# A hybrid decoder layer on one core: the modulation's sums over partitions moved behind the next projection, their stream given its own slots, and one half projection moved forward

## The chip, the core and the metric

One core of a Trainium2 chip runs the whole layer as one program. The metric is the device time of one execution in microseconds (us); below it is better. PE is TensorE, DVE VectorE, ACT ScalarE, POOL GpSimd, and SP the engine that issues the DMAs.

## What is computed

The layer takes a sequence `x` of 1024 tokens by 1024 features and a conditioning vector `c`. The reference, cut to what matters here:

```python
mod = (c @ w_c + b_c).reshape(B, 6, D)
shift_m, scale_m, gate_m, shift_f, scale_f, gate_f = mod      # rows m = 0 to 5
u = x * (1.0 + scale_m) + shift_m
fq, fk, fv, ff, gq, gk, gv, ga, gr = split(u @ w_in)
fox_out = fox_attention(fq, fk, fv, ff, b_f)
gla_out = gla_attention(gq, gk, gv, ga, w_a2, b_a, gr, g_gla)
y = concatenate([fox_out, gla_out]) @ w_o
x = layer_norm(ALPHA * x + (1.0 + gate_m) * y, ln1_g, ln1_b)
u2 = x * (1.0 + scale_f) + shift_f
x = layer_norm(ALPHA * x + (1.0 + gate_f) * (silu(u2 @ w_gate) * (u2 @ w_up)) @ w_down, ln2_g, ln2_b)
```

All of it is float32. The kernel keeps that precision by splitting each operand into a high and a low part and multiplying three times (high by high, high by low, low by high).

## The kernel before

The work is unrolled in Python: a first stage computes the rows m = 0 and 1 of the modulation, the scaled input `u` (split into `uh` and `ul`) and part of the projections; then come the other projections, the linear heads (GLA), the softmax heads (FoX), the mixer and the feed-forward part.

**The projections in question.** `proj_tok` (L316) loads the weights of some columns in two halves with `load_split` (L90): a DMA on SP into a tile of kind `raw` (L92), a cast to the high part on ACT (L87), a subtraction for the low part on DVE (L88). `raw`, `hi` and `lo` are kinds of tiles with three buffers each. Then it runs over the eight token tiles in two groups of four banks, three matmuls for each of the eight blocks of features (L330 to L332), and evacuates. It is called four times in a row: gv0 and gv1 (264 columns each), gr0 and gr1 (256 each; their evacuation is the `gr` activation of L410).

**The rest of the modulation.** Between these calls stands `mod_rest(m)` for m = 2 to 5 (L339). It streams eight tiles of `w_c` (L343) through slots 35 to 37 and accumulates them on DVE, weighted by `c` (L345, L347), into slot 28 or 29. The accumulated tile is split into slots 37 and 35. Four matmuls with a column of ones (L359, L360, tile `mps`, banks b6 and b7) then sum over the partitions; the result is copied by ACT (L366; for m = 2 and 5 added to `b_c` on DVE, L362) to the tile `grow` in slot 32 and stored to the HBM tensor `grow_d` (L367). After `mod_rest(5)`, `mod_cols` (L369) loads the rows of m = 3 and 4 back into a `raw` tile (L371) and transposes them into columns (L373, tile `mcs`, bank b7).

**After the projections.** The low-rank gate input is transposed (L460, `gaps`, banks b6 and b7); `gla_prep` for two pairs of heads makes the decayed operands on DVE, ACT and POOL; then eight steps of `gla_pair` run, each for both pairs (among others the transposition `kt`, L534). The fq and fk projections of the softmax heads come in half projections, `units`, of 24 matmuls: two are called before the steps, and one behind each step while there are any (eight in all).

**What sets the order.** The framework takes the order of the program as priority. It simulates the program, and each engine gets its instructions in the order in which they are ready there, earlier ones in the program first. So a matmul may stand in PE's queue in front of others that precede it in the program. On the chip every queue is worked in order. A tile of a kind waits for a free buffer of that kind. `tc.issue_after(ins)` puts an instruction behind `ins` in the queue of its engine, without a wait for its end. The helper `after(key)` (L175) does that for the instruction remembered in `last[key]`.

Of the kernel before, what the change touches and what calls it, by code (L numbers as in the profile page):

```python
# [9 lines left out]
F32R = mybir.dt.float32r  # L10
# [8 lines left out]
NK = D // P  # L19
# [14 lines left out]
def hymba_layer_kernel(  # L34
# [21 lines left out]
    nc = tc.nc  # L56
# [13 lines left out]
    def nm(s):  # L70
        uid[0] += 1
        return f"{s}_{uid[0]}"

    def slot(i, shape=(1024,), dt=F32, name="t"):
        return sp.tile([P, *shape], dt, tag=f"s{i}", name=nm(name))

    def bank(tag, name="ps"):
        return pp.tile([P, 512], F32, tag=tag, name=nm(name))
# [7 lines left out]
    def split(dst_hi, dst_lo, src):  # L86
        nc.scalar.copy(dst_hi, src)  # L87
        return nc.vector.tensor_tensor(dst_lo, src, dst_hi.bitcast(F32), op=ALU.subtract).ins  # L88

    def load_split(shape, src):  # L90
        raw = wtile("raw", shape, F32)
        nc.sync.dma_start(raw, src)  # L92
        hi = wtile("hi", shape, F32R)
        lo = wtile("lo", shape, F32R)
        split(hi, lo, raw)
        return hi, lo
# [11 lines left out]
    ones_r = cp.tile([P, 1], F32R, name="ones_r")  # L108
# [28 lines left out]
    uh, ul = [], []  # L137
# [35 lines left out]
    last = {}  # L173

    def after(key):  # L175
        return tc.issue_after(last[key]) if key in last else nullcontext()
# [104 lines left out]
    for m in range(3):  # L281
        dst = [gq[0], gq[1], gk[0]][m]
        for h in range(2):
            hs = slice(h * 512, (h + 1) * 512)
# [9 lines left out]
    def pbank(n=4):  # L294
        pb[0] += 1
        return bank(f"b{pfirst[0] + pb[0] % n}", "acc")
# [19 lines left out]
    def proj_tok(col, n, nb, evac):  # L316
        ws = []
        for g in range(2):
            wv = w_in[g * 512 : (g + 1) * 512, col : col + n].rearrange("(k p) n -> p k n", p=P)
            ws.append(load_split((4, n), wv))  # L320
        per = 4 if nb >= 4 else 1
        for t0 in range(0, NT, per):
            pss = [pbank(nb) for _ in range(per)]
            for g in range(2):
                wh, wl = ws[g]
                for i in range(per):
                    ts = slice((t0 + i) * P, (t0 + i + 1) * P)
                    ps = pss[i][:, 0:n]
                    for k in range(4 * g, 4 * g + 4):
                        nc.tensor.matmul(ps, uh[k][:, ts], wh[:, k % 4, :], start=k == 0, stop=False)  # L330
                        nc.tensor.matmul(ps, uh[k][:, ts], wl[:, k % 4, :], start=False, stop=False)  # L331
                        nc.tensor.matmul(ps, ul[k][:, ts], wh[:, k % 4, :], start=False, stop=k == NK - 1)  # L332
            for i in range(per):
                evac(t0 + i, pss[i])

# [3 lines left out]
    def mod_rest(m):  # L339
        acc = slot(28 + m % 2, name="wacc")  # L340
        for k in range(NK):
            raw = slot(35 + k % 3, name="wc")
            nc.sync.dma_start(raw, w_c[k * P : (k + 1) * P, m * D : (m + 1) * D])  # L343
            if k == 0:
                nc.vector.tensor_scalar(acc, raw, ccol[:, 0:1], None, op0=ALU.mult)  # L345
            else:
                nc.vector.scalar_tensor_tensor(  # L347
                    acc, raw, ccol[:, k : k + 1], acc, op0=ALU.mult, op1=ALU.add
                )
        row = slot(32, name="grow")  # L350
        if m in (2, 5):
            nc.sync.dma_start(row[0:1, :], b_c[m * D : (m + 1) * D].rearrange("(o n) -> o n", o=1))
        hi = slot(37, dt=F32R, name="ah")
        lo = slot(35, dt=F32R, name="al")
        split(hi, lo, acc)
        for h in range(2):
            hs = slice(h * 512, (h + 1) * 512)
            ps = bank(f"b{6 + h}", "mps")
            nc.tensor.matmul(ps[0:1, :], ones_r, hi[:, hs], start=True, stop=False)  # L359
            nc.tensor.matmul(ps[0:1, :], ones_r, lo[:, hs], start=False, stop=True)  # L360
            if m in (2, 5):
                nc.vector.scalar_tensor_tensor(  # L362
                    row[0:1, hs], ps[0:1, :], 1.0, row[0:1, hs], op0=ALU.add, op1=ALU.add
                )
            else:
                nc.scalar.copy(row[0:1, hs], ps[0:1, :])  # L366
        nc.sync.dma_start(grow_d[m - 2 : m - 1, :], row[0:1, :])  # L367

    def mod_cols():  # L369
        rows = wtile("raw", (P,), F32)[0:16]  # L370
        nc.sync.dma_start(rows, grow_d[1:3, :].rearrange("m (k p) -> (m k) p", p=P))  # L371
        ps = bank("b7", "mcs")
        nc.tensor.transpose(ps[:, 0:16], rows, ident[0:16, 0:16])  # L373
        nc.vector.tensor_tensor(mcol[:, 2, :], ps[:, 0:8], cols[:, 24:32], op=ALU.add)
        nc.vector.scalar_tensor_tensor(mcol[:, 3, :], ps[:, 8:16], 1.0, cols[:, 32:40], op0=ALU.add, op1=ALU.add)

        nc.vector.tensor_tensor(mcol[:, 4, :], vcol[:, 16:24], mcol[:, 3, :], op=ALU.mult)
        nc.vector.tensor_tensor(mcol[:, 4, :], mcol[:, 2, :], mcol[:, 4, :], op=ALU.add)
        nc.vector.tensor_tensor(mcol[:, 5, :], mcol[:, 3, :], vcol[:, 8:16], op=ALU.mult)
# [12 lines left out]
    def evac_gv1(t, ps):  # L392
        nc.scalar.copy(gv_t(t)[:, 264:512], ps[:, 0:248])
        nc.scalar.copy(ga_tok[:, t, :], ps[:, 248:264])

    proj_tok(C_GV, 264, 4, evac_gv0)
    mod_rest(3)
    proj_tok(C_GV + 264, 264, 4, evac_gv1)
    mod_rest(4)

    gr = [slot(24 + i, (2, 512), name="gr") for i in range(4)]
# [3 lines left out]
    def gr_t(t):  # L405
        return gr[t // 2][:, t % 2, :]

    def evac_gr(h):
        def f(t, ps):
            nc.scalar.activation(gr_t(t)[:, h * 256 : (h + 1) * 256], ps[:, 0:256], AF.Silu)  # L410
            if h == 1:
                nc.gpsimd.tensor_tensor(gr_t(t), gr_t(t), ggb, op=ALU.mult)
        return f

    proj_tok(C_GR, 256, 4, evac_gr(0))
    mod_rest(5)
    mod_cols()
    proj_tok(C_GR + 256, 256, 4, evac_gr(1))


    def log_sigmoid(pss, bias, t0, t1, t2, n=P):
# [35 lines left out]
    for h in range(2):  # L457
# [3 lines left out]
        hs = slice(h * 512, (h + 1) * 512)  # L461
# [4 lines left out]
    def ch(t, i):  # L466
        return t.rearrange("p (n c t) -> p n c t", c=2, t=64)[:, :, i, :]
# [5 lines left out]
    def gla_prep(p):  # L473
        aps = []
        for h in range(2):
            hs = slice(h * 512, (h + 1) * 512)
            ps = bank(f"b{4 + h}", "aps")
            nc.tensor.matmul(ps, wa2[:, p * P : (p + 1) * P], gaT[0:80, hs], start=True, stop=True)
            aps.append(ps)
        t0, t1, t2 = gtmp[p]  # L480
        log_sigmoid(aps, vcol[:, p : 1 + p], t0, t1, t2)
        nc.vector.tensor_tensor_scan(t1, rmask, t0, 0.0, op0=ALU.mult, op1=ALU.add)
        bl = t1.rearrange("p (n t) -> p n t", t=64)[:, :, 63:64]
        nc.scalar.activation(t0, t1, AF.Exp, scale=1.0 / GATE_TEMP)
        nc.vector.tensor_tensor(gq[p], gq[p], t0, op=ALU.mult)
        nc.scalar.activation(t2, t1, AF.Exp, scale=-1.0 / GATE_TEMP)
        nc.vector.tensor_tensor(t2, gk[p], t2, op=ALU.mult)
        nc.scalar.activation(dec[:, p, :], bl.rearrange("p n t -> p (n t)"), AF.Exp, scale=1.0 / GATE_TEMP)
        nc.vector.tensor_tensor(
            t0.rearrange("p (n t) -> p n t", t=64),  # L490
            bl.broadcast_to([P, 16, 64]),
            t1.rearrange("p (n t) -> p n t", t=64),
            op=ALU.subtract,
        )
        nc.scalar.activation(t0, t0, AF.Exp, scale=1.0 / GATE_TEMP)
        nc.vector.tensor_tensor(gk[p], gk[p], t0, op=ALU.mult)
        d2 = dec[:, p, :].rearrange("p (n c) -> p n c", c=2)
        nc.vector.tensor_tensor(dec12[:, p, :], d2[:, :, 0], d2[:, :, 1], op=ALU.mult)
        nc.gpsimd.tensor_scalar(ch(t1, 0), ch(gk[p], 0), 1.0, 1.0, op0=ALU.mult, op1=ALU.mult)
        nc.gpsimd.tensor_scalar(ch(t1, 1), ch(t2, 1), 1.0, 1.0, op0=ALU.mult, op1=ALU.mult)  # L500
        nc.gpsimd.tensor_tensor(
            ch(gk[p], 0), ch(gk[p], 0), d2[:, :, 1:2].broadcast_to([P, 8, 64]), op=ALU.mult
        )
        nc.gpsimd.tensor_scalar(ch(t0, 0), ch(gq[p], 0), 1.0, 1.0, op0=ALU.mult, op1=ALU.mult)
        nc.gpsimd.tensor_tensor(
            ch(t0, 1), ch(gq[p], 1), d2[:, :, 0:1].broadcast_to([P, 8, 64]), op=ALU.mult
        )
# [68 lines left out]
    units = qk_units(0) + qk_units(1)  # L576
    gla_prep(0)
    units.pop(0)()
    gla_prep(1)
    units.pop(0)()  # L580
    for n in range(NT):
        for p in range(2):
# [27 lines left out]
    for h in range(2):  # L610
        ps = bank(f"b{h}", "fps")
# [813 lines left out]
```

## Time and profile before

| | |
|---|---|
| time, median of 3 runs | 1285.75 us (1284.23 to 1287.79) |
| the profiled execution, its own time | 1285.78 us |
| its span from first to last instruction | 1283.8 us |
| mean granted clock of TensorE | 0.99 of full speed |
| busy: PE, DVE, ACT, POOL | 96%, 63%, 40%, 20% of the span |

The span is cut into what each engine did and what ended its waits. An engine that is idle costs time only if the engine that sets the end waits for it. The granted clock is the share of TensorE's full clock in a stretch: 1.00 is 2.4 GHz, 0.50 is 1.2 GHz.

### The profile page before, as it was taken

To read this page: it belongs to the slowest core of one execution; us is meant where nothing else is said; L and a number is where in the kernel's file an instruction comes from. 1 tells how busy PE (TensorE), PEld (TensorE's weight loads), DVE (VectorE), ACT (ScalarE), POOL (GpSimd) and SP (SyncE) were. 2 spreads that over 40 slices of the span, in tenths; PEclk is the share of its full clock that TensorE was granted. 3 is DMA by queue.
4 is the path that set the end of the run, shared out by engine and by line. 5 is a ranking of instruction groups with operands and counts; after the bars stand their busy time and mean duration, and the time that the engine had idled before them with its cause. 6 is when DMAs were issued, how large, how long until landed. Compare 5 with 4: busy or idle time off the path is not lost.

```text
span 1283.8 us, 16487 instructions
## 1 busy us (share of the span) xinstructions
PE 1230.5 (96%) x6209; PEld 995.2 (78%) x6209; DVE 805.5 (63%) x1180; ACT 516.7 (40%) x876; POOL 254.2 (20%) x252
## 2 busy tenths in 40 slices
PE   5999999999999999998979999999999999999986
PEld 4889997889877756666758888888888887887875
DVE  7656538641456357548876666656656659585698
ACT  3422346422345356645732332333333344344341
POOL 3500033230344345412000000000000016061014
PEclk9999999999999999999989999999999999999999
DMA  9865612111123324224354454435544458775571
GB/s 299 258 215 191 214 52 65 25 26 38 62 91 107 119 49 115 92 91 131 116 165 166 160 185 176 164 124 178 183 140 142 166 200 279 236 239 189 190 236 66
DMA packets 137295, 190.66 MB, mean 149 GB/s; under 512 B 7952, under 2 KB 87930, under 8 KB 137216
## 3 DMA queue, kind: packets, MB, share of 16 engines
q1 hardware_dynamic: 137216, 189.61, 44.8%
q8 instruction: 49, 0.80, 0.3%
q14 instruction: 30, 0.25, 0.1%
HBM read 140.94 MB, written 44.32 MB: 144 GB/s over the span
## 4 chain that ended last, share of the span: by engine, by line
PE 79%; DVE 7%; DMA 5%; ACT 3%; POOL 3%; issue 2%; SPq 1%; POOLq 0%; DVEq 0%; ACTq 0%
PE ga L1009 18%; PE dn L1194 16%; PE gc L1009 9%; PE gb L1009 4%; PE pv L791 4%; DMA wc<-in_w_c_dram 3%; PE tr L781 3%; PE acc L330 3%; PE acc L332 3%; PE acc L331 3%; PE acc L100 2%; PE acc L101 2%; PE acc L99 2%; PE sc L751 1%; PE sc L752 1%
## 5 line engine op out<-in xcount | busy, mean ns | idle before, releaser
L88 DVE TENSOR_TENSOR lo<-raw,hi 128x1024 fp32r<-128x1024 f32 (+1 forms) x112 | 146.7, 1310 | 99.3 <-ACT hi L87 90.2
L87 ACT CAST hi<-raw 128x1024 fp32r<-128x1024 f32 (+1 forms) x112 | 114.6, 1025 | 116.9 <-PE ga L1009 52.7
L1227 POOL TENSOR_TENSOR r<-r,l1g 128x1024 f32<-128x1024 f32 x8 | 24.5, 3079 | 492.2 <-DMA r<-z_d 440.9
L1009 PE MATMUL ga<-s,hi 128*128 128x512 f32 x344 | 109.2, 398 | 7.7 <-ACT hi L87 7.0
L1194 PE MATMUL dn<-hi,ah 128*128 128x512 f32 x280 | 111.1, 397 | 4.0 <-DVE dc L1268 3.5
L1194 PE MATMUL dn<-lo,ah 128*128 128x512 f32 x280 | 110.5, 395 | 1.4 <-DVE lo L88 1.4
L1194 PE MATMUL dn<-hi,al 128*128 128x512 f32 x280 | 109.9, 394 | 0.0
L330 PE MATMUL acc<-hi,uh 128*128 128x264 f32 (+1 forms) x384 | 108.8, 284 | 0.9 <-ACT m L531 0.8
L332 PE MATMUL acc<-hi,ul 128*128 128x264 f32 (+1 forms) x384 | 108.7, 284 | 0.0
L331 PE MATMUL acc<-lo,uh 128*128 128x264 f32 (+1 forms) x384 | 108.7, 283 | 0.0
L88 DVE TENSOR_TENSOR al<-ar,ah 128x1024 fp32r<-128x1024 f32 (+1 forms) x38 | 56.8, 1498 | 48.4 <-ACT ah L87 48.1
L1009 PEld LDWEIGHTS ga<-s,hi 128*128 128x128 f32 x344 | 65.6, 191 | 24.0 <-ACT hi L87 7.4
L87 ACT CAST ah<-ar 128x1024 fp32r<-128x1024 f32 (+1 forms) x38 | 37.3, 983 | 102.3 <-PE dn L1194 91.8
L330 PEld LDWEIGHTS acc<-hi,uh 128*128 128x128 f32 x384 | 72.8, 190 | 2.3 <-ACT m L531 1.0
L331 PEld LDWEIGHTS acc<-lo,uh 128*128 128x128 f32 x384 | 72.8, 190 | 0.6 <-issue 0.2
L332 PEld LDWEIGHTS acc<-hi,ul 128*128 128x128 f32 x384 | 72.7, 190 | 0.4
L756 DVE CUSTOM_DVE_ANT_0 pr<-sc,smask 128x128 f32<-128x128 f32 (+7 forms) x64 | 47.6, 754 | 37.6 <-PE sc L752 22.6
L1009 PE MATMUL ga<-s,lo 128*128 128x512 f32 x172 | 68.6, 400 | 0.0
L1194 PEld LDWEIGHTS dn<-hi,ah 128*128 128x128 f32 x280 | 53.1, 190 | 17.1 <-issue 3.9
L1009 PE MATMUL gc<-s,b 128*128 128x512 f32 x264 | 63.8, 390 | 0.5 <-DVE hf L1114 0.5
L786 ACT COPY pt<-tr 128x512 f32<-128x512 f32 x80 | 45.6, 582 | 45.6 <-PE tr L781 38.6
L1194 PEld LDWEIGHTS dn<-lo,ah 128*128 128x128 f32 x280 | 52.9, 189 | 13.8 <-DVE lo L88 1.8
(350 smaller groups left out, 2960.0 us busy)
## 6 DMA issues: line engine op xcount, KB each, us to landing
ar<-a_d SPq DMA_DIRECT2D x35, 512.0 KB, 4.4
wc<-in_w_c_dram SPq DMA_DIRECT2D x32, 512.0 KB, 4.4
raw<-in_w_gate_dram SPq DMA_DIRECT2D x25, 512.0 KB, 4.1
wd<-in_w_down_dram SPq DMA_DIRECT2D x22, 512.0 KB, 5.8
t_d<-wd SPq DMA_DIRECT2D x22, 512.0 KB, 4.8
a_d<-hf SPq DMA_DIRECT2D x22, 512.0 KB, 2.8
u<-in_w_up_dram SPq DMA_DIRECT2D x21, 512.0 KB, 4.1
raw<-t_d SPq DMA_DIRECT2D x20, 512.0 KB, 5.3
```

The costliest lines, as they stand in the source:

```text
L87: nc.scalar.copy(dst_hi, src)
L88: return nc.vector.tensor_tensor(dst_lo, src, dst_hi.bitcast(F32), op=ALU.subtract).ins
L99: nc.tensor.matmul(ps, lh, rh, start=start, stop=False)
L330: nc.tensor.matmul(ps, uh[k][:, ts], wh[:, k % 4, :], start=k == 0, stop=False)
L331: nc.tensor.matmul(ps, uh[k][:, ts], wl[:, k % 4, :], start=False, stop=False)
L332: nc.tensor.matmul(ps, ul[k][:, ts], wh[:, k % 4, :], start=False, stop=k == NK - 1)
L756: nc.vector.tensor_tensor_reduce(t[:, 0:nk], sc[:, 0:nk], smask[:, S - nk : S], op0=ALU.add, op1=ALU.min, scale=-1.0, scalar=3e38, accum_o ...
L781: nc.tensor.transpose(tr[:, a * 256 + j * P : a * 256 + (j + 1) * P], ps_[2 * j + par][:, (2 * kk + a) * P : (2 * kk + a + 1) * P], ident,)
L786: nc.scalar.copy(pt[:, par, :], tr)
L791: nc.tensor.matmul(pv[64 * par : 64 * par + 64, 0:256], fv_t(kb)[:, 64 * h : 64 * h + 64], pt[:, par, a * 256 : (a + 1) * 256], start=kb == 0,
L1009: ins = nc.tensor.matmul(ps, x, y, start=start and j == 0 and i == 0, stop=j == NJ - 1 and i == 2, skip_group_check=not start,)
L1194: last["dn"] = nc.tensor.matmul(ps, x[:, a, qs], y[:, a, :], start=start and a == 0 and i == 0, stop=stop and a == n - 1 and i == 2, skip_ ...
```

## The change

The four matmuls of a sum are taken out of `mod_rest` into `mod_row(m)`, which is called one projection later: `mod_row(2)` behind gv0, `mod_row(3)` behind gv1, `mod_row(4)` behind gr0 and in front of `mod_rest(5)` and `mod_cols`, `mod_row(5)` behind gr1. The first matmul of each bank is queued behind the last matmul of that projection. The copies and the store of the row move with it. The split goes into slots 30 and 31, so that slots 35 and 37 hold the `w_c` stream alone. And one more half projection is called in front of the linear heads' steps.

```diff
-                        nc.tensor.matmul(ps, ul[k][:, ts], wh[:, k % 4, :], start=False, stop=k == NK - 1)
+                        last["proj"] = nc.tensor.matmul(
+                            ps, ul[k][:, ts], wh[:, k % 4, :], start=False, stop=k == NK - 1
+                        ).ins
...
-        hi = slot(37, dt=F32R, name="ah")
-        lo = slot(35, dt=F32R, name="al")
+        hi = slot(30, dt=F32R, name="ah")
+        lo = slot(31, dt=F32R, name="al")
         split(hi, lo, acc)
+        rows_[m] = (row, hi, lo)
+
+    rows_ = {}
+
+    def mod_row(m):
+        row, hi, lo = rows_[m]
         for h in range(2):
             hs = slice(h * 512, (h + 1) * 512)
             ps = bank(f"b{6 + h}", "mps")
-            nc.tensor.matmul(ps[0:1, :], ones_r, hi[:, hs], start=True, stop=False)
+            with after("proj"):
+                nc.tensor.matmul(ps[0:1, :], ones_r, hi[:, hs], start=True, stop=False)
             nc.tensor.matmul(ps[0:1, :], ones_r, lo[:, hs], start=False, stop=True)
...
     proj_tok(C_GV, 264, 4, evac_gv0)
+    mod_row(2)
     mod_rest(3)
     proj_tok(C_GV + 264, 264, 4, evac_gv1)
+    mod_row(3)
     mod_rest(4)
...
     proj_tok(C_GR, 256, 4, evac_gr(0))
+    mod_row(4)
     mod_rest(5)
     mod_cols()
     proj_tok(C_GR + 256, 256, 4, evac_gr(1))
+    mod_row(5)
...
     gla_prep(1)
     units.pop(0)()
+    units.pop(0)()
     for n in range(NT):
```

## Rows read from the trace of the kernel before

**Rows 1.** The page: busy time, share of the span and instructions of PE.

```profile
PE 1230.5 (96%) x6209; PEld 995.2 (78%) x6209; DVE 805.5 (63%) x1180; ACT 516.7 (40%) x876; POOL 254.2 (20%) x252
```

**Rows 2.** Who PE waited for: us in total, times, longest us.

```profile
PE ga L1009 <- ACT hi L87: 7.0, 1, 7.0
...
PE mps L359 <- ACT ah L87: 3.9, 2, 2.4
...
PE kt L534 <- POOL gk L501: 2.5, 1, 2.5
```

**Rows 3.** PE's timeline: start us, us, instruction, count, idle before and its releaser.

```profile
83.70 0.64 PE L359 MATMUL mps<-ah,ones_r 128*1 128x512 f32 x2 [2.43 <-ACT ah L87]
...
129.64 0.62 PE L359 MATMUL mps<-ah,ones_r 128*1 128x512 f32 x2 [1.48 <-ACT ah L87]
```

**Rows 4.** Windows: busy us (count) of each engine, clock, DMA share, GB/s.

```profile
84.00:88.00 4.00, 4.00 (x20) 3.45 (x19) 2.18 (x3) 0.26 (x1) 0.00 (x0) 0.57 0.92 312
...
128.00:132.00 4.00, 2.52 (x19) 1.93 (x18) 1.69 (x2) 1.95 (x6) 0.00 (x0) 1.00 0.51 140
...
216.00:220.00 4.00, 3.74 (x12) 2.98 (x13) 4.00 (x6) 1.73 (x3) 0.82 (x2) 0.68 0.01 2
220.00:224.00 4.00, 4.00 (x20) 3.08 (x20) 1.59 (x3) 1.04 (x3) 2.37 (x4) 0.89 0.41 131
```

**Rows 5.** SP's queue in order of time, 132 to 139.

```profile
132.85 0.24 SPq L367 DMA_DIRECT2D grow_d<-grow  x1
...
136.12 0.31 SPq L371 DMA_DIRECT2D raw<-grow_d  x1
137.90 0.35 SPq L343 DMA_DIRECT2D wc<-in_w_c_dram  x1
138.29 0.98 SPq L92 DMA_DIRECT2D raw<-in_w_in_dram  x2
```

**Rows 6.** DVE's timeline: the subtractions that free gr0's and gr1's first raw buffers.

```profile
105.58 1.22 DVE L88 TENSOR_TENSOR lo<-raw,hi 128x1024 fp32r<-128x1024 f32 x1
...
125.90 1.22 DVE L88 TENSOR_TENSOR lo<-raw,hi 128x1024 fp32r<-128x1024 f32 x1
...
144.50 1.23 DVE L88 TENSOR_TENSOR lo<-raw,hi 128x1024 fp32r<-128x1024 f32 x1 [1.24 <-ACT hi L87]
```

**Rows 7.** Tile raw, 40 to 240: count, duration ns min/median/max, first and last start.

```profile
L371 SPq DMA_DIRECT2D raw<-grow_d x1: 313/313/313, 136.1 to 136.1; - x1
...
L373 PE MATMUL mcs<-ident,raw x1: 231/231/231, 160.1 to 160.1; 16*128 16x16 f32 x1
```

**Rows 8.** ACT's timeline: row copies, the cast of gr1's weights, gr0's last-but-one evacuation.

```profile
131.77 1.05 ACT L366 COPY grow<-mps 1x512 f32<-1x512 f32 x2 [1.50 <-issue]
...
143.42 1.05 ACT L87 CAST hi<-raw 128x1024 fp32r<-128x1024 f32 x1 [3.97 <-DMA raw<-in_w_in_dram]
...
150.79 0.39 ACT L410 ACTIVATE gr<-acc 128x256 f32<-128x256 f32 x1 [1.05 <-PE acc L332]
```

**Rows 9.** Who SP's queue waited for, 60 to 240: us in total, times, longest.

```profile
SPq L343 <- PE mps L360: 3.4, 3, 1.7
...
SPq L352 <- DMA grow_d<-grow: 2.7, 1, 2.7
```

**Rows 10.** Loads of L92 issued in 120 to 170: time from issue to landing.

```profile
DMA to landing us min/median/max: 3.7/3.7/6.1
```

**Rows 11.** Windows of 1 us behind the 7.0 us wait of ga: first and last.

```profile
652.00:653.00 1.00, 0.96 (x2) 0.50 (x2) 1.00 (x3) 0.20 (x1) 0.00 (x0) 0.50 0.00 0
...
657.00:658.00 1.00, 1.00 (x4) 0.76 (x4) 0.92 (x1) 0.00 (x0) 0.00 (x0) 0.61 1.15 323
```

**Rows 12.** Tile mps: the additions on DVE, duration ns min/median/max.

```profile
L362 DVE SCALAR_TENSOR_TENSOR grow<-mps,grow x4: 668/670/679, 86.7 to 157.9; 1x512 f32<-1x512 f32 x4
```

**Rows 13.** ACT's timeline: evacuations of the first and the sixth half projection.

```profile
183.54 0.60 ACT L309 ACTIVATE fq<-acc 128x512 f32<-128x512 f32 x1 [3.90 <-PE acc L101]
...
215.81 0.59 ACT L309 ACTIVATE fq<-acc 128x512 f32<-128x512 f32 x1
```

## The prediction

> **What bounds the kernel now.** I read the page first, then who PE waited for, then PE's timeline around the longest of those waits, then the granted clock in windows around them, and last SP's queue and the casts that feed PE. The page shows a kernel that lives on PE: it is busy 96% of the span [rows 1], so time can be won only where PE stands still or runs at the lower clock. The waits of PE are few [rows 2]. Two of them, 3.9 us together, are the sums over partitions of the modulation (`mps`, L359), which stand in PE's queue before the operand they read has been cast. In the timeline the first takes 2.43 us (PE goes on at 83.70) and the second 1.48 us (at 129.64) [rows 3]. The clock tells what follows: behind the first stall the granted clock is 0.57 in 84 to 88, so part of that stretch ran at 1.2 instead of 2.4 GHz; behind the second it stays at 1.00 [rows 4]. A third wait of 2.5 us is that of the first linear-head step for `gk` from POOL (`kt`, L534) [rows 2], with 0.68 and 0.89 in 216 to 224 behind it [rows 4].
>
> Look then at SP's queue between 132 and 139 [rows 5]. The sum rows of m=3 and m=4 are stored to HBM (L367) and read back (L371) into a tile of the rotating kind `raw`, which has three buffers. Directly behind L371 (one w_c load, which waited for its slot, stands between) come the two loads of the weights of the last projection, gr1 (L92 at 138.29, two issues within 0.98 us). Nothing was missing for these but their place: the `raw` buffers that they take had been free since the subtractions that began at 105.58 and 125.90 and last 1.2 us [rows 6]. So buffers of a kind are handed out in program order: gr1's first weight tile is taken after the `rows` tile of `mod_cols`, and that only when L371 can be issued. The bank b7 shows the same: the rows were loaded from 136.1 on, but their transposition `mcs` ran only at 160.1 [rows 7], after the sums of m=5, which come earlier in program order and use b7 too. Today this order costs nothing. gr1's weights are cast at 143.42 [rows 8] and subtracted at 144.50 [rows 6], ready at 145.7, and gr0 (the projection in front) ends one tile (0.39 + 1.05 us) after the evacuation at 150.79 [rows 8], so at 152.2: a slack of 6.5 us.
>
> **The change, part by part.** The sum is made against the profiled execution: span 1283.8, its own time 1285.78 us, which is the median of the runs (1285.75) within 0.03.
>
> *Sums behind the projection.* No instruction is added: four sums, four matmuls each, before and after. What goes is the waiting: 2.43 and 1.48 us [rows 3], and the clock behind the first, 4 us x (1 - 0.57) = 1.72 us [rows 4]. Together -5.63 us. Since the sums now stand a whole projection later, their operands are there. Nothing is late in their place: the next projection's weights are cast during the one before.
>
> *Slots 30 and 31 for the split.* SP's w_c loads (L343) no longer wait for the sums to free their slot (3.4 us) [rows 9], nor for the split before them. The stream ends earlier, but nobody except the sums waits for it: 0. New is that the cast of the next m into slot 30 waits for the sums of the last one. A cast is 1.05 us, an evacuation 0.39 with 1.05 idle before it [rows 8], and PE needs a bank again only four tiles on: 0, at most 1.1.
>
> *Row 4 behind gr0, in front of mod_cols.* This is where I expect the price. The store of row 4 is now released by sums that stand behind gr0's last matmul. L371 needs that store, and gr1's loads stand behind L371. When gr0 and the four sums are through, PE has nothing: gr1 lacks its weights, the later projections come after it for `raw` buffers, the transpositions of the gate input wait for banks b6 and b7 behind the sums of m=5. Step by step, from the end of the sums to gr1's first pair of matmuls: the two row copies on ACT 1.1 (131.77, 1.05) [rows 8]; store to L371 136.12 - 132.85 = 3.27 [rows 5]; L371 to the first L92 0.35, since its issue takes 0.31 and the w_c load between them is gone by then [rows 5]; landing of 512 KB 4.5, an estimate between the median 3.7 [rows 10] and the 5.1 that lie between the issue at 138.29 and the cast at 143.42; the cast 1.05 [rows 8]; the subtraction 1.23 [rows 6]. That is 11.5 us of idle PE. It is at least 10.7 (landing 3.7) and at most 13.1 (landing 6.1) [rows 10]. The DMA of the sums' row is tiny, so its 2.7 us of waiting [rows 9] is latency that nothing shortens.
>
> The Trainium skill, page "DMA: Bandwidth & Descriptors", section "Anatomy of one DMA — SWDGE (gpsimd) path", gives about 2.0 us of fixed cost for a DMA, most of it the write receipt; by it the store would cost about 1.0 us less than the row says, and the net below would be +7.2 instead of +8.2 us. The row is used, as it is the same store in the same queue.
>
> Then the clock. Behind the 7.0 us wait of `ga` [rows 2] it is 0.50 in five windows of 1 us from 652 on and 0.61 in the sixth [rows 11]: at most 2.9 us lost, part of which was idle. Behind 2.4 us of idle it was 1.72. I take 2.3. The step costs 11.5 + 2.3 = +13.8 us. `mcs` falls into the gap and costs nothing.
>
> *Row 5 behind gr1.* Its four matmuls only move. But the transpositions behind it need banks b6 and b7, which two DVE additions now have to read first. That holds up the gate chain of the linear heads by some 1.7 us (two additions of 0.67 [rows 12], plus the sums' own pass). PE meanwhile does the half projections of fq and fk: 0, at most +1.7.
>
> *Third half projection.* The eight half projections are the same work. In the trace the first is evacuated at 183.54 and the sixth at 215.81 [rows 13], before the first step's `kt` at 216, so the third already runs ahead of every step. The edit asks for what happens anyway: 0. Should it shift the order so that `kt` no longer waits, 2.50 + 4 x (0.32 + 0.11) = 4.2 us are won; a loss, by a later start of the chain, is the same 1.7 as above.
>
> **Sum:** -5.63 + 13.8 = +8.2 us, 1294.0 us. Its own bounds: 10.7 + 1.7 - 5.6 = +6.8 without any mishap; 13.1 + 2.9 - 5.6 + 1.7 = +12.1 at the worst, 1297.9.
>
> **The rivals.** *Gain without the price* (the other side): gr1's loads go out ahead of L371, because a free `raw` buffer goes to whoever can use it. Its place is SP's queue at the end of gr0; it decides if the first L92 of gr1 is issued more than 7 us (landing, cast and subtraction) before gr0's last matmul. Then PE never stops and -5.63 remains: 1280.2. For it speaks that loads do pass blocked ones in this queue; against it that gr1's loads stood behind L371 with buffers free for 31 us [rows 5, 6], and `mcs` behind sums that were not ready [rows 7]. 0.15.
>
> *Price, but `kt` won too:* the shifted chain and the third half projection take the `kt` stall away. +8.2 - 4.2 = +4.0, with the shorter landing +2.6: 1288.4 to 1289.8, on the border of what can be told from no change. For it: the stall is an ordering matter. Against: `kt` waits for POOL, which the edit does not touch. 0.09.
>
> *The edit is not obeyed* (the sums stay where they were): 1285.8. Each first matmul is tied to the projection's last one, on the same engine, so 0.02.
>
> **How the numbers follow.** The slower case has 0.74, the gain without the price 0.15, the two others 0.11, of which the `kt` case is counted as no change for most of its share. About 0.3% (3.9 us) is what a measurement of this kernel can tell from no change. Faster 0.15, same 0.10, slower 0.75. The range goes from 1285, which takes in the two middle cases, to 1298; only the faster rival and the slower case's tail are left out, under 0.2. The slower case alone is 1292.6 to 1297.9.
>
> **What would show it.** Right: PE's waits name no `mps` any more; PE has one wait of about 11 us at `acc` L330 or L331 for a cast or a subtraction, right behind the sums of m=4, with the clock at 0.5 behind it; in SP's queue L371 still stands in front of gr1's two L92, some 3.3 us behind the store of row 4. The w_c stream ends earlier. Wrong: gr1's L92 early in the queue and PE dense from 75 to 180 (then the faster rival), or a wait of `mps` left. The step I trust least is the order in which `raw` buffers are given out; then the landing time.

## The result and the profile after

The changed kernel takes 1298.16 us (median of 5 runs, 1295.01 to 1302.57) against 1287.79 us for the kernel before on the same chip: a ratio of 1.0089 [1.0072, 1.0106], some 11 us slower. The forecast was 1294.0, a ratio of 1.0064, with a range up to 1298.0: the sign and the main mechanism were right, the size lies 0.16 us above the range. Of the 4.2 us between 1294.0 and 1298.16, 2.0 are the kernel before itself, whose median is 1287.79 here and was 1285.75 in the runs from which the forecast started. The profiled execution took 1295.01 us with a span of 1293.2; it is the fastest of the five, so its rows show the cost rather too small. One kernel among the experiments (GpSimd's order changed alone) ran at two levels, four of its six executions about 30 us longer than the fastest; its ratio rests on the two others, and nothing is concluded from its time.

The page of the kernel after, busy times, answers to [rows 1]; PE has the same number of instructions, is busy 4.0 us longer, and of the 9.4 us by which the span has grown it is idle in 5.4:

```profile
PE 1234.5 (95%) x6209; PEld 997.0 (77%) x6209; DVE 803.3 (62%) x1180; ACT 517.8 (40%) x876; POOL 255.1 (20%) x252
```

Who PE waited for in the kernel after (us in total, times, longest), against [rows 2]. Lines have moved: L343 is L345 now, L347 L349, L352 L354, L359 L368, L367 L376, L371 L380, L373 L382 and L534 L547.

```profile
PE ga L1023 <- ACT hi L87: 7.0, 1, 7.0
...
PE mcs L382 <- DMA raw<-grow_d: 4.9, 1, 4.9
PE kt L547 <- POOL gk L514: 3.6, 1, 3.6
...
PE acc L330 <- ACT hi L87: 3.5, 1, 3.5
```

The waits of `mps` are gone. In their place stand 4.9 us for the rows read back from HBM and 3.5 us for a cast, and `kt` waits 3.6 instead of 2.5 us. PE's timeline of the kernel after (start, length, instruction, idle before and its releaser) shows that the first two are one gap:

```profile
129.49 0.39 PE L331 MATMUL acc<-lo,uh 128*128 128x256 f32 x1 [1.14 <-DVE lo L88]
...
147.28 0.39 PE L369 MATMUL mps<-al,ones_r 128*1 128x512 f32 x1
152.57 0.26 PE L382 MATMUL mcs<-ident,raw 16*128 16x16 f32 x1 [4.90 <-DMA raw<-grow_d]
156.29 1.22 PE L330 MATMUL acc<-hi,uh 128*128 128x256 f32 x4 [3.46 <-ACT hi L87]
157.55 0.58 PE L331 MATMUL acc<-lo,uh 128*128 128x256 f32 x1
```

The sums of m=4 end at 147.28 + 0.39 = 147.67, and gr1 goes on in full at 157.55, 9.88 us later; between them lie one transposition and four matmuls that need the high part alone. The first row is another wait, not in the forecast. SP's queue and ACT's timeline in that gap tell what it is made of:

```profile
149.31 0.24 SPq L376 DMA_DIRECT2D grow_d<-grow  x1
150.57 0.23 SPq L354 DMA_DIRECT2D grow<-in_b_c_dram  x1
150.85 0.31 SPq L380 DMA_DIRECT2D raw<-grow_d  x1
151.20 0.97 SPq L92 DMA_DIRECT2D raw<-in_w_in_dram  x2
```

```profile
147.29 0.57 ACT L375 COPY grow<-mps 1x512 f32<-1x512 f32 x1
147.77 1.04 ACT L87 CAST ah<-wacc 128x1024 fp32r<-128x1024 f32 x1
148.72 0.57 ACT L375 COPY grow<-mps 1x512 f32<-1x512 f32 x1
155.19 1.04 ACT L87 CAST hi<-raw 128x1024 fp32r<-128x1024 f32 x1 [5.91 <-DMA raw<-in_w_in_dram]
```

As before [rows 5], gr1's loads (L92) stand right behind the read-back (L380), and now this is where PE waits. DVE's timeline has the two subtractions, gr0's at 128.21 behind an accumulation of the w_c stream, and gr1's at 156.27:

```profile
127.01 1.28 DVE L349 SCALAR_TENSOR_TENSOR wacc<-wc,cols,wacc 128x1024 f32<-128x1024 f32 x1 [1.42 <-DMA wc<-in_w_c_dram]
128.21 1.22 DVE L88 TENSOR_TENSOR lo<-raw,hi 128x1024 fp32r<-128x1024 f32 x1
...
156.27 1.23 DVE L88 TENSOR_TENSOR lo<-raw,hi 128x1024 fp32r<-128x1024 f32 x1 [2.76 <-ACT hi L87]
```

Windows of the kernel after (busy us and count of PE, PEld, DVE, ACT, POOL, then granted clock, DMA share, GB/s), first around the gap:

```profile
148.00:152.00 4.00, 0.00 (x0) 0.00 (x0) 1.23 (x1) 1.28 (x2) 0.00 (x0) 0.74 0.01 4
152.00:156.00 4.00, 0.26 (x1) 0.18 (x1) 0.61 (x5) 0.81 (x1) 0.00 (x0) 0.50 0.89 266
156.00:160.00 4.00, 3.68 (x15) 3.38 (x16) 3.34 (x5) 1.28 (x2) 0.00 (x0) 0.50 0.33 82
160.00:161.00 1.00, 1.00 (x10) 1.00 (x9) 0.00 (x0) 0.00 (x0) 0.00 (x0) 0.91 1.06 267
```

```profile
84.00:88.00 4.00, 4.00 (x35) 4.00 (x34) 2.87 (x4) 0.77 (x3) 0.00 (x0) 1.00 0.90 287
...
228.00:232.00 4.00, 4.00 (x13) 3.14 (x12) 2.78 (x4) 1.64 (x2) 0.62 (x1) 0.57 0.00 0
```

The 0.57 at 84 to 88 of [rows 4] is gone, as forecast. Behind the gap the clock is 0.50 up to 160, and behind the wait of `kt` it is 0.57.

### The profile page after: what moved, and what is told of

It is laid out like the page before. It is cut to its first block, busy times and chain, and to the rows that moved or that the text cites. A ratio compares the mean times of both kernels' runs of the same rounds, so it can differ in the third digit from the quotient of the medians.

```text
span 1293.2 us, 16478 instructions
## 1 busy us (share of the span) xinstructions
PE 1234.5 (95%) x6209; PEld 997.0 (77%) x6209; DVE 803.3 (62%) x1180; ACT 517.8 (40%) x876; POOL 255.1 (20%) x252
## 4 chain that ended last, share of the span: by engine, by line
PE 77%; DVE 9%; DMA 6%; ACT 3%; POOL 2%; issue 2%; SPq 1%; POOLq 0%; DVEq 0%; ACTq 0%
PE ga L1023 18%; PE dn L1208 16%; PE gc L1023 9%; DMA wc<-in_w_c_dram 5%; PE gb L1023 4%; PE pv L805 4%; PE tr L795 3%; PE acc L331 2%; PE acc L330 2%; PE acc L332 2%; PE acc L100 2%; PE acc L101 2%; PE acc L99 2%; PE sc L765 1%; PE sc L766 1%
```

## The experiments

Ratios are to the kernel before, about 1287 us on the same chip in the same session, so 0.001 is 1.3 us. A difference between two ratios has about 0.003, or 4 us, of uncertainty; where a price is small the waits of the profile stand beside it. A second measure is the start of the first evacuation of `fv`, the projection that follows the linear heads (275 us before): all parts of the change lie ahead of it, and what comes behind it, which no edit touches, takes 1008 to 1014 us in the profiles of these kernels.

**The changed kernel again**, as the base of what follows.

> The changed kernel once more, beside the others, to see what a second profile of it keeps. All theories: a ratio of 1.0075 to 1.0105. In the trace PE idle for 9 to 10 us between the sums of m=4 and the last projection, in two waits (mcs for grow_d, then acc for the cast). If the 1.2 us that the first profile shows more behind 1056 us than in front of it belong to the change, they stay; if they are only where the low clock falls, the stretch at 0.5 near the end has another length in this profile.

Measured: 1299.47 us, 1.0085 [1.0062, 1.0108]. The gap is the same (4.8 + 3.4 us of waiting), the wait for gr0's low part is 2.4 us here against 1.14 above, with 0.63 in 132 to 136 behind it, and behind the 3.6 us of `kt` the clock is 0.81, 0.50 and 0.83 in 228 to 240, against the one window of 0.57 above.

**The rows in a tile of their own.** One line: the read-back takes a free slot and no buffer of the kind `raw`.

```diff
-        rows = wtile("raw", (P,), F32)[0:16]
+        rows = slot(33, (P,), name="mrows")[0:16]
```

> The rows of mod_cols go into slot 33 instead of a raw buffer; nothing else. Theory 1 (raw buffers are given out in program order, so the last projection's weights stand behind the read-back of the rows): the two loads go out some 25 us earlier, the gap of 9.6 us of idle and 1 us of low clock is gone, ratio about 0.998 (the 5.6 us of the old stalls won, less 1.1 for the new wait in gr0 and 2 for the chain of the linear heads). Theory 2 (PE's order: the transposition mcs stands in front of the projection and waits for the round trip over HBM): mcs is now placed inside the projection, so most of the gap goes here too. Theory 3 (the loads are late for another reason, such as SP or the DMA): the gap stays, 1.008.

Measured: 1287.47 us, 0.9995 [0.9978, 1.0012]; 1.0085 - 0.9995 = 0.0090, or 11.6 us, come back. SP's queue of this kernel shows gr1's two loads, 40 to 50 us earlier than in the changed kernel:

```profile
101.35 0.38 SPq L92 DMA_DIRECT2D raw<-in_w_in_dram  x1
...
110.67 0.38 SPq L92 DMA_DIRECT2D raw<-in_w_in_dram  x1
```

What PE still waits for in this kernel, and the window behind the second of these waits:

```profile
PE kt L547 <- POOL gk L514: 3.6, 1, 3.6
PE acc L331 <- DVE lo L88: 2.0, 1, 2.0
```

```profile
132.00:136.00 4.00, 4.00 (x23) 4.00 (x23) 3.23 (x3) 0.77 (x2) 0.31 (x1) 0.61 0.13 50
```

Nothing of the gap is left, though the read-back goes out even later than in the changed kernel (156.18 against 150.85). The cause is thus the buffer, not the row's way through HBM. But the ratio is only back at 1: the 5.63 us that the moved sums should give are missing.

**The transposition alone moved.** The read-back stays where it is; `mcs` and its additions are issued behind gr1 and the sum of row 5.

```diff
-    mod_cols()
+    rows_t = mod_cols()
     proj_tok(C_GR + 256, 256, 4, evac_gr(1))
     mod_row(5)
+    mod_cols_t(rows_t)
```

> The changed kernel with the read-back of the rows where it is, in a raw buffer, but its transposition mcs called behind the last projection and the sums of m=5. Theory 1 (order of the raw buffers): the gap stays whole, one wait of about 9.5 us of acc for the cast and the subtraction, ratio 1.008 to 1.010. Theory 2 (mcs in PE's queue is what waits): its 4.9 us go, ratio about 1.005.

Measured: 1300.86 us, 1.0111 [1.0082, 1.014]. The gap stays, now as one wait of 8.5 us for the cast:

```profile
PE acc L330 <- ACT hi L87: 8.5, 1, 8.5
```

So `mcs` in front of gr1 in PE's queue was a passenger: without it the cast ends no sooner. The ratio lies above the 1.008 to 1.010 of theory 1, by less than its interval; a stop of 2.2 us at the linear heads' `o` with the clock at 0.50 in 236 to 252 behind it, as in the next run, was not in that theory.

**The whole of `mod_cols` moved** behind gr1 and the sum of row 5, read-back included.

```diff
-    mod_cols()
     proj_tok(C_GR + 256, 256, 4, evac_gr(1))
     mod_row(5)
+    mod_cols()
```

> The changed kernel with the whole of mod_cols called behind the last projection and the sums of m=5, so that its raw buffer is asked for after those of the projection. Theory 1: the gap goes, about 0.998, as with the own tile; the small weight w_a2 now stands behind the read-back, which has long been possible by then, so no new wait. Theory 2: the same. Theory 3: the gap stays.

Measured: 1293.06 us, 1.0049 [1.0028, 1.007]. The gap is gone, as in the run with its own tile, but the expected 0.998 is missed: 0.0054 or 6.9 us more is lost than there. The profile has 2.2 us of waiting of the linear heads' `o` for DVE that the run with its own tile has not, and behind it the clock stays low for some 16 us:

```profile
224.00:228.00 4.00, 2.07 (x9) 1.62 (x10) 3.23 (x5) 3.10 (x6) 1.35 (x2) 0.85 0.01 2
228.00:244.00 16.00, 15.80 (x62) 11.93 (x61) 7.03 (x24) 4.48 (x21) 5.46 (x7) 0.51 0.12 33
```

That is at most 4 x 0.15 + 16 x 0.49 = 8.4 us, where the run with its own tile loses 4 x 0.43 = 1.7 behind `kt` (0.57 in 220 to 224). The difference covers what is missing. Why `o` waits here was not taken further.

**Slots 30 and 31 alone**, in the kernel before.

```diff
-        hi = slot(37, dt=F32R, name="ah")
-        lo = slot(35, dt=F32R, name="al")
+        hi = slot(30, dt=F32R, name="ah")
+        lo = slot(31, dt=F32R, name="al")
```

> The kernel before with one part of the change alone: the cast and the low part of each modulation row (ah, al) take slots 30 and 31 in place of 37 and 35, so the w_c stream has slots 35 to 37 to itself; the sums over partitions stay where they were, and no third half projection. Theory A (the prediction's: nobody but the sums waits for the stream): the two mps waits stay at about 2.4 and 1.5 us, maybe shorter, no other wait appears, ratio 0.998 to 1.001. Theory B (the stream runs ahead, and its accumulations of row 5 stand before the low part of gr0's second half in VectorE's queue): a wait of 1 to 2.7 us of a matmul acc<-lo,uh (128x256) on the DVE low part near 125 to 132 us, in one profile with half clock behind it, ratio 1.000 to 1.004. B is shown by that wait, A by its absence.

Measured: 1290.29 us, 1.0015 [1.0001, 1.0029]. Neither theory as it stood: the wait of B is absent, yet its first half is there, and A's "no other wait" does not hold, since two waits for a bank (0.9 us at 117.84 and 1.3 us at 141.85, each until an evacuation on ACT) are new. The low part of gr0's second half comes at 129.15, against 125.90 [rows 6], behind the accumulations that the freed slots let through. DVE's timeline of this kernel:

```profile
127.95 1.28 DVE L347 SCALAR_TENSOR_TENSOR wacc<-wc,cols,wacc 128x1024 f32<-128x1024 f32 x1 [0.17 <-DMA wc<-in_w_c_dram]
129.15 1.22 DVE L88 TENSOR_TENSOR lo<-raw,hi 128x1024 fp32r<-128x1024 f32 x1
```

PE simply isn't there yet: in this kernel it is still held back by earlier stalls (2.6 us at `mps`, 0.9 at a bank), and the four matmuls of a sum in front of gr0 start at 126.65. With the moved sums they start 5 us earlier (121.59 in the kernel with VectorE's order mended, below), and PE meets the late low part. So the wait seems to take both parts of the change; a kernel with the sums moved and the slots left was not run. Up to `fv` the profile is not slower but 1.6 us faster than before (273.36 against 274.92).

**The third half projection alone**, in the kernel before.

```diff
     gla_prep(1)
     units.pop(0)()
+    units.pop(0)()
     for n in range(NT):
```

> The kernel before with another part alone: a third half projection in front of the linear heads' steps. Theory A (the prediction's: the projection lies in front of the steps instead of between them, and the GpSimd product that kt waits for starts and ends when it did): the kt wait goes or shrinks, and what it gives is lost again where the last step has no half projection left beside it; ratio 0.998 to 1.001. Theory B (the wait is not reached by it, because the scheduler sets the third half projection behind the first kt anyway): the kt wait stays at 2.5 us or more, ratio 0.9995 to 1.0005, order on TensorE nearly as before. Theory C (the half projection missing between the last steps costs idle time of TensorE): new waits behind o or kv of the late steps, 1.001 to 1.004.

Measured: 1288.16 us, 1.001 [0.9993, 1.0027]. The evacuations of all half projections and of the first `o` come 0.12 to 0.15 us later than before, which is no change of order, and the wait of `kt` is the same 2.5 us as in [rows 2]. Theory B holds: the half projections ran ahead of the steps anyway. The clock behind `kt` is 0.57 in 216 to 220 here; with the slots alone, behind the same 2.5 us, it was 1.00.

**VectorE's order.** Beside the rows' own tile, the accumulations of m=5 are queued behind the low part of gr0's second half (`psplit` is the last subtraction of `load_split`).

```diff
-        split(hi, lo, raw)
+        last["psplit"] = split(hi, lo, raw)
...
-                nc.vector.scalar_tensor_tensor(
-                    acc, raw, ccol[:, k : k + 1], acc, op0=ALU.mult, op1=ALU.add
-                )
+                with after("psplit") if m == 5 else nullcontext():
+                    nc.vector.scalar_tensor_tensor(
+                        acc, raw, ccol[:, k : k + 1], acc, op0=ALU.mult, op1=ALU.add
+                    )
```

> The changed kernel with the row read-back in a slot of its own (as in the run with its own tile, ratio 0.9995) and, beside it, the accumulations of row 5's w_c stream queued on VectorE behind the low part of gr0's second half. Theory B (that order costs TensorE 2.0 us and the half clock behind it): the wait acc<-lo,uh on the DVE low part near 130 us falls under 0.5 us, no half clock near 131 us, 2 to 3.7 us less than with the tile alone: ratio 0.9965 to 0.998. Rival (the wait is set by the weights' transfer that lands late, or the stream made later only delays row 5, its chain into the linear heads, and kt): the wait stays near 2 us, or it goes and the wait on kt or on the linear heads grows by as much; ratio 0.999 to 1.001.

Measured: 1282.91 us, 0.9979 [0.9961, 0.9996]. The wait and the 0.61 behind it are gone (1.00 in 132 to 136), since the subtraction of gr0's second half, which began at 129.31 in the kernel with the rows' own tile, now stands ahead of the stream in DVE's timeline:

```profile
121.03 1.22 DVE L88 TENSOR_TENSOR lo<-raw,hi 128x1024 fp32r<-128x1024 f32 x1
```

The ratios give 0.0016 or 2.1 us for it, which their uncertainty alone could make; up to `fv` the profiles give 3.9 us (274.97 and 271.06), close to the 2.0 us of the wait and 4 x (0.04 + 0.39) = 1.7 of the clock in 128 to 136. The wait of `kt` stays at 3.6 us. The next three kernels ask why.

**Four repairs at once**: in addition the sum of row 5 is called behind the transposition of the gate input, and GpSimd's product of `gk` goes ahead of the two products of `gq`.

```diff
     proj_tok(C_GR + 256, 256, 4, evac_gr(1))
-    mod_row(5)
...
+    mod_row(5)
+
     def ch(t, i):
...
-        nc.gpsimd.tensor_tensor(
+        gks = nc.gpsimd.tensor_tensor(
             ch(gk[p], 0), ch(gk[p], 0), d2[:, :, 1:2].broadcast_to([P, 8, 64]), op=ALU.mult
-        )
+        ).ins
+        with tc.issue_after(gks):
...
```

> The changed kernel with four repairs: the row read-back in a slot of its own, row 5's accumulations behind the low part of gr0's second half on VectorE, the sum of row 5 traced behind the transposition of the gate columns (so it doesn't hold the PSUM banks in front of them), and the GpSimd product of gk, which kt waits for, queued ahead of the two products of gq. Theory (three waits on the path into the linear heads are repaired, each alone): kt wait under 1 us in place of 3.6, no half clock near 220 us, 3 to 5 us less than with the first two repairs: ratio 0.993 to 0.996, faster than both kernels. Rival (the linear heads' chain is bound elsewhere: gk's product itself runs later because GpSimd waits for the exponentials, or the first o step waits for the products of gq now made later): the kt wait goes over into a wait of at or o of the same length; ratio 0.9965 to 0.999.

Measured: 1280.31 us, 0.9947 [0.9928, 0.9966], faster than both kernels, and no wait of `kt` shows any more.

**Row 5 late, GpSimd's order as it was.** The first hunk of the last diff alone, on the kernel with VectorE's order mended.

> The kernel of the run with VectorE's order mended (ratio 0.9979) with the sum of row 5 traced behind the transposition of the gate columns, and GpSimd's order left as it was. Theory (the sum of row 5 behind gr1 delays the gate chain: its PSUM banks and its place on TensorE hold the gaps transpositions, which in that run began 6.2 us after gr1's last eviction instead of 1.2 us as before): gaT is written some 5 us earlier, the first GpSimd product at about 198.5 in place of 203.6, and the kt wait falls from 3.6 to at most 2.5 us; ratio 0.994 to 0.9965. Rival (GpSimd's order of products is the cause, since the product that kt waits for comes last of five there): kt wait stays at 2.5 to 3.6 us and the ratio at 0.997 to 0.999.

Measured: 1278.47 us, 0.9944 [0.9925, 0.9964]: the same as all four repairs, so GpSimd's order is not needed. The wait of `kt` falls to 1.1 us:

```profile
PE kt L549 <- POOL gk L516: 1.1, 1, 1.1
```

Where it comes from is read in PE's timeline. First the kernel with VectorE's order mended, the last matmul of row 5's sum, the last of 21 matmuls of a half projection behind it (L99 to L101) and the gate input's transposition:

```profile
169.74 0.40 PE L370 MATMUL mps<-al,ones_r 128*1 128x512 f32 x1
...
174.62 0.40 PE L99 MATMUL acc<-uh,hi 128*128 128x512 f32 x1
174.85 1.04 PE L474 MATMUL gaps<-ident,ga_tok 128*16 128x128 f32 x8
```

and, from DVE's timeline, the two additions that free the banks:

```profile
169.70 1.27 DVE L372 SCALAR_TENSOR_TENSOR grow<-mps,grow 1x512 f32<-1x512 f32 x2 [3.74 <-PE mps L370]
```

then PE in the kernel with row 5 late:

```profile
168.86 1.03 PE L473 MATMUL gaps<-ident,ga_tok 128*16 128x128 f32 x8
176.75 0.40 PE L369 MATMUL mps<-ah,ones_r 128*1 128x512 f32 x1
```

gr1's last evacuation begins within 0.2 us in both (169.25 and 169.06), the transposition 6.0 us earlier in the second. Counted from that start it is 5.6 us late in the first and 0.2 us early in the second, as it was before (175.89 and 176.09); the expectation has 6.2 and 1.2 us for the first and for the kernel before. The chain behind it follows: GpSimd's first product starts at 203.62 in the one and 198.18 in the other, 5.4 us earlier.

**GpSimd's order alone**, on the kernel with VectorE's order mended.

> The same kernel (VectorE's order mended) with GpSimd's order alone changed: the product of gk, which kt waits for, ahead of the two products of gq; row 5's sum stays directly behind gr1. Theory (row 5's sum delays the whole gate chain): the first GpSimd product stays near 203.6, the kt wait only falls by the products passed, 3.6 us, and what it gives turns partly into a wait of at or o on products of the same chain; ratio 0.9955 to 0.998. Rival (GpSimd's order is the cause): kt wait gone without another in its place, ratio 0.994 to 0.9955, as with all four repairs (0.9947).

Measured: 1310.77 us median; the ratio of 1.0005 [0.9957, 1.0052] tells nothing (two executions, as said above). In its profile GpSimd's first product stands at 203.64, so the gate chain is as late as it was, and the 3.6 us of `kt` have become 1.6 of `kt` and 1.3 of `o`: the turn that the theory expected. What it is worth in time stays open. What made the profiled execution so long is not that wait of `o` itself, in PE's timeline,

```profile
226.19 0.49 PE L544 MATMUL o<-gv,gbuf 128*128 128x128 f32 x2 [1.28 <-DVE gbuf L538]
```

but the clock behind it, in the windows of the same kernel:

```profile
224.00:228.00 4.00, 2.72 (x17) 1.97 (x16) 3.22 (x9) 1.35 (x6) 0.84 (x2) 1.00 0.23 51
228.00:232.00 4.00, 4.00 (x15) 3.23 (x15) 1.93 (x8) 1.06 (x6) 0.69 (x1) 0.55 0.27 80
240.00:260.00 20.00, 20.00 (x67) 16.14 (x65) 7.28 (x25) 5.22 (x22) 3.79 (x5) 0.50 0.06 13
260.00:280.00 20.00, 20.00 (x65) 16.05 (x64) 7.73 (x27) 5.15 (x23) 4.04 (x6) 0.50 0.07 14
280.00:296.00 16.00, 15.54 (x50) 12.63 (x51) 7.15 (x21) 4.71 (x20) 5.69 (x7) 0.50 0.08 17
296.00:300.00 4.00, 4.00 (x32) 4.00 (x32) 2.06 (x6) 0.38 (x1) 1.78 (x3) 0.92 0.07 17
```

**VectorE's order taken back**, row 5 late kept: the fastest kernel without the edge to `psplit`.

> The changed kernel with two of the three repairs of the fastest kernel (ratio 0.9944): the row read-back in a slot of its own and the sum of row 5 behind the gate columns' transposition; VectorE's order left as in the change. Theory (the three prices add: read-back 11.6 us, low part 2 us, row 5 4.5 us): the wait acc<-lo,uh on the DVE low part near 130 us is back at about 2 us, no kt wait over 1.5 us, ratio 0.9955 to 0.9975. Rival (the low part's wait is taken up later, so it needs no repair): ratio 0.9935 to 0.995.

Measured: 1283.78 us, 0.9979 [0.9963, 0.9994], 0.0035 or 4.5 us more than with it, and just above the 0.9955 to 0.9975 of the theory. The wait is back, 3.4 us here, with 0.61 behind it:

```profile
PE acc L331 <- DVE lo L88: 3.4, 1, 3.4
```

```profile
132.00:136.00 4.00, 4.00 (x23) 4.00 (x23) 3.24 (x4) 0.41 (x2) 0.00 (x0) 0.61 0.29 112
```

3.4 + 4 x (1 - 0.61) = 5.0 us, and every evacuation from 146 to 314 us stands 4.95 to 4.97 us later than in the fastest kernel. The two repairs together won 6.6 us (0.9995 to 0.9944), each alone 2.1; with 0.003 of uncertainty in each difference that is as far as the ratios go. Up to `fv` the profiles give 8.9 us for both (274.97 and 266.12), 3.9 for each alone, and 4.9 or 5.0 for the one that comes second.

**The fastest kernel without the third half projection.**

> The fastest kernel (ratio 0.9944) without the third half projection in front of the linear heads' steps. Theory (the third half projection changes nothing, as in the run of that part alone): ratio 0.993 to 0.996, the evacuations of the half projections at the same times to 0.3 us, kt wait about 1.1 us. Rival (with the gate chain early, the half projection in front is what fills TensorE until the first kt): the kt wait or an at wait grows by 2 us or more, ratio 0.996 to 0.999.

Measured: 1278.98 us, 0.9948 [0.9931, 0.9964], all evacuations of the half projections 0.20 to 0.22 us earlier, a shift that begins long before them; `kt` waits 1.0 us. The third half projection does nothing here either.

## Why the prediction was right and wrong

**Right: the gain.** Both stalls of the sums and the 0.57 behind the first are gone. The kernel with three repairs, which keeps the moved sums, is 0.0056 or 7.2 us faster than before; up to `fv` its profile is 8.8 us ahead. ACT's timeline, first before, then in that kernel:

```profile
274.92 0.38 ACT L598 COPY fv<-acc 128x264 f32<-128x264 f32 x1 [2.47 <-POOL rms L551]
```

```profile
266.12 0.38 ACT L614 COPY fv<-acc 128x264 f32<-128x264 f32 x1 [2.47 <-POOL rms L566]
```

The term of 5.63 and what `kt` gave make as much: its wait fell from 2.5 to 1.1 us, with no lower clock in 216 to 232 any more, so 5.63 + 1.4 + 1.7 = 8.8. How the term is split is not fixed: with the third half projection alone, the sums where they were, the waits at `mps` are 4.8 us and the clock behind them stays at 1.00.

**Right: the order of the buffers**, the step that I trusted least. gr1's loads stood behind the read-back, as the order in SP's queue [rows 5] and the idle buffers [rows 6] had suggested, and one line that takes the read-back out of `raw` gave 11.6 us back. The rival "gain without the price" fell, and so did the two small ones: `kt` waits 3.6 us instead of 2.5, and no wait of `mps` is left.

**Mis-sized: the term of +13.8.** In the profile it is 9.88 us, less 0.5 for the four matmuls done in it (in gr0 they follow each other every 0.12 us), plus the clock behind it: (160.0 - 157.55) x 0.5 + 1 x 0.09 = 1.3. That makes 10.7; the runs say 11.6, with about 3.7 of uncertainty. Step by step, forecast against measured: the row copies up to the store 1.1 against 149.31 - 147.67 = 1.64, since the cast of m=5's sum stood between them on ACT; store to read-back 3.27 against 150.85 - 149.31 = 1.54; to the first L92 0.35 and 0.35; landing 4.5 against 155.19 - 151.20 = 3.99; the cast up to the subtraction 1.05 against 1.08; subtraction up to the matmul 1.23 against 1.28. The clock was 2.3 against 1.3, because part of the half clock fell on an idle PE.

The largest miss is the store. I wrote that its 2.7 us of waiting "is latency that nothing shortens". It was not: the row load behind it went out 2.98 us after the store in the kernel before (135.83 against 132.85, with the DMA engines 0.77 busy in 133 to 136) and 150.57 - 149.31 = 1.26 us after it here, where they are 0.01 busy. Other kernels have the same pair: 1.22 us with slots 30 and 31 alone (0.01 busy in that stretch), 3.04 us with VectorE's order mended (0.67 busy). The row was taken from a busy stretch and used in an empty one. The Trainium skill, page "DMA: Bandwidth & Descriptors", section "Latency and other measured facts", says that the latency of HBM grows with its load and makes up most of a DMA's fixed cost; this trace agrees in direction. The 2.0 us that I quoted from the Trainium skill (the same page, section "Anatomy of one DMA — SWDGE (gpsimd) path", so for DMAs issued from GpSimd, while this store is issued from SP) and set aside lie between the two measurements.

**Wrong: "Nothing is late in their place".** This is the first of the two steps that put the time above the range. The sentence, and the 0 for slots 30 and 31 ("nobody except the sums waits for it"), hid a term. The stream waits in the same in-order queue of DVE as the subtraction that makes gr0's low part. With its slots free it was queued further ahead of that subtraction, with the sums gone from in front of gr0 PE came earlier, and PE waited 1.14 to 2.4 us in the changed kernel and up to 3.4 with others repaired. Behind the stops of 2.0, 2.3, 2.4 and 3.4 us the clock fell to 0.61 to 0.67, behind one of 2.7 us (the transposition alone moved) it stayed at 1.00. The repair was worth 2.1 us in one pair of kernels and 4.5 in the other by the ratios, 3.9 and 5.0 up to `fv`. I had looked at who waits for the stream's result, not at who stands behind it.

**Wrong in size: row 5 behind gr1, "0, at most +1.7".** This is the second. I counted the two additions and the sums' own pass. They take from 169.05 to 170.97 in the kernel with VectorE's order mended, 1.9 us, as said. But the transposition then starts only at 174.85: it has a place in PE's queue that was fixed in advance, behind matmuls of the half projections, and loses 3.9 us more. The gate chain came 5.4 us later there, and taking this away was worth 0.0035 or 4.5 us (4.9 up to `fv`). In the changed kernel against the one before, it shows as 3.6 instead of 2.5 us at `kt`; the clock behind it cost as much as before (4 x 0.43 us in the one window against 4 x (0.32 + 0.11)).

**Right: the third half projection at 0**, alone in the kernel before and again in the fastest one.

**The sum.** The change cost 1.0085 in its second run, 10.9 us: -5.63 for the stalls, +11.6 for the buffer, and the remaining 5 falls to the two terms that I had at 0. The two profiles of the changed kernel show 2.2 us for these in the first (1.14 for the low part, 1.1 more at `kt`) and 6.9 in the second (2.4 for the low part, 1.1 more at `kt`, and 1.7 more of clock behind each). That the size missed by only some 3 us, beside the 2.0 by which the kernel before itself ran longer, is luck: a gap forecast 2 to 3 us too long stood against them. The range ended at 1298 because its upper bound added only known costs at their worst (12.1 us); the two terms taken as 0 had bounds of 1.1 and 1.7 in the text, while the measured repairs were worth 2.1 to 4.5 each by the ratios and 3.9 to 5.0 up to `fv`.

## What to carry to other kernels

A load can wait for a buffer that is free: where tiles of a kind are given out in program order, a tile that can't be loaded yet holds up every later load of its kind, so a late, tiny read-back belongs in a tile of its own. When a stream is given more slots, look not only for who needs its result but for who stands behind it in its engine's queue; and when work is moved in front of a short chain, remember that the chain's first instruction has a fixed place in the queue and may lose far more than the work itself takes.

## What the hardware showed that was not expected

The length of a short stop of PE does not fix whether the clock falls behind it, nor for how long. It was 0.61 behind 2.0 us in the kernel with the rows' own tile and 0.57 behind 2.43 us before, but stayed 1.00 behind 1.48 us before, 1.14 us after, and 2.7 us in the kernel with the transposition alone moved. Behind the same 2.5 us at `kt` it was 0.68 and 0.89 before, 0.57 with the third half projection alone and 1.00 with the slots alone. So a term for the clock behind such a stop is a guess: at `kt` the same wait cost 0 to 1.7 us of it.

In the linear heads' steps it stayed low for longer. Behind 2.2 us at `o` it was 0.50 or 0.51 for 16 us in two kernels (`mcs` alone moved, 236 to 252; all of `mod_cols` moved, 228 to 244). In the run with GpSimd's order changed it fell behind a stop of 1.28 us at `o`, to 0.55 in 228 to 232, and was then 0.50 up to 296, while from 240 on PE counts as busy all but 0.46 us of 56; there it rose again only when the projections behind the linear heads began. The fastest kernel does the same steps at 1.00. Why it stayed low stays open.
